# Starting the gathered rows beside the routing, and dealing the rest evenly over the rows of V

## The chip, the cores and the metric

The kernel runs on one core of one Trainium2 chip. Its time is the device time of one execution in microseconds (us); the text before the change has a median of 2013.02 us over three runs (2002.75 to 2023.59). Five engines work side by side, each through its own list of instructions in order: PE (matmul), DVE (elementwise, vector), ACT (activation), POOL (general purpose, also the queue from which indirect gathers are issued) and SP (a queue for plain DMA). An instruction that waits holds up everything behind it on its engine.

## The reference

One layer of a hybrid attention model over 512 latent tokens and 256 context tokens, width 1024, float32. The part that matters here is its last, the PEER expert block. Each token picks, in each of 8 heads, 16 of 16384 experts by product keys, and the block adds up 128 expert outputs for each token:

```python
def block(t):                                   # 128 tokens at a time
    q = (t @ wq).reshape(PEER_BLOCK, PEER_HEADS, 2, PEER_DQ // 2)
    s = jnp.einsum('tpcd,pckd->tpck', q, sub_keys).astype(jnp.float32)
    s1, i1 = lax.top_k(s[:, :, 0], PEER_TOPK)
    s2, i2 = lax.top_k(s[:, :, 1], PEER_TOPK)
    ...                                         # 16 x 16 sums, top 16 of them: idx, top
    g = jax.nn.softmax(top, axis=-1)
    a = jax.nn.gelu(jnp.einsum('tpkd,td->tpk', u[idx], t).astype(jnp.float32), approximate=False)
    return jnp.einsum('tpk,tpkd->td', (g * a).astype(t.dtype), v[idx])
```

`u` and `v` are 16384 x 1024. Ahead of it stand the input projection, neighbourhood attention with a recurrence beside it, and the output projection; behind it a gated residual and an RMSNorm. None of those is touched.

## The kernel before, in words

The first 630 us (projections, mixers, output projection) are left alone by the change. From there on the expert block is one program (`experts`) that treats two groups of tokens in two ways.

- **Tokens 0 to 383, dense.** All 16384 experts are worked through in 128 *rows* of 128 experts. `Activations.step` is one row of U h: the 128x1024 piece of U (`uraw`, fetched two rows at a time) is split into a high and a low part (`uhi` on ACT L66, `ulo` on POOL or DVE L69), PE multiplies both with the tokens in 24 matmuls of 384 columns (`ua`, L396, L397, L399), and ACT applies Gelu (`act`). A row of V is 18 matmuls of 512 columns into `acc` (L555). Its weights are `W` (the softmax weights spread out over experts and tokens) times `act`: POOL multiplies (`w`, L535), ACT and DVE split (`wh`, `wl`), and V itself is split too (`vhi` on ACT, `vlo` on DVE).
- **Tokens 384 to 511, gathered.** For each of 128 slots (8 heads x 16) a 128x1024 tile of rows of U is gathered by index (`rows<-u,gidx`, L417, POOL), DVE takes its dot product with the tokens (L422); after Gelu, the same for rows of V, which DVE adds to `gacc` (L434). These 256 gathers, with `GLAG` = 3 more calls to empty the queue, are 259 *slots* of the generator `gathered`. There are four buffers of `rows`, and a gather is issued three slots ahead of its use. Gathers, dots and sums are kept in program order.

The stages: *retrieval* (`Retrieval.run`: scores and top 16; three steps of U h behind each of the first seven heads), *routing* (`Routing.block`, twelve blocks of 32 tokens, which make `W`: for each of eight groups of four tokens DVE writes one-hot tiles `hot` and `hg` in 16 bit, L348 and L351, PE multiplies them into `wo`, L356, ACT copies them out to `stage`, and SP writes a block's 2 MB to DRAM), then the loop over the *rows of V*, c = 0 to 127. In that loop a row takes a step of U h with it when `up.n < c + 2 * (AHEAD - 1)`, that is while the finished rows of U h are fewer than c + 16; rows with a step are called mixed here, rows without one plain. Rows of U h finished before the loop are spilled to DRAM and fetched back.

What sets the order: a scheduler places each instruction on its engine's list by program order, readiness and its own estimates, and may pull work ahead (steps of the next routing blocks stand before the end of the retrieval on PE). Only what is marked with `keep_in_program_order` keeps the order of the text among itself.

Of the kernel before, what the change touches and what calls it, by code (L numbers as in the profile page):

```python
# [32 lines left out]
P = 128  # L33
# [10 lines left out]
PH, NK, TOPK = 8, 128, 16  # L44
# [114 lines left out]
GRP = 4  # L159
# [250 lines left out]
def gathered(tc, a, pool, gp, idx, weight, h, acc):  # L410

    nc = tc.nc
    dots = pool.tile([P, P], F32, name="dots")

    def rows(src, s):
        t = gp.tile([P, D], F32, name="rows")
        tc.keep_in_program_order(nc.gpsimd.indirect_dma_start(  # L417
            out=t[:], out_offset=None, in_=a[src], in_offset=bass.IndirectOffsetOnAxis(ap=idx[:, s:s + 1], axis=0)))
        return t

    def dot(t, s):
        tc.keep_in_program_order(nc.vector.tensor_tensor_reduce(  # L422
            out=t, in0=t, in1=h, op0=ALU.mult, op1=ALU.add, scale=1.0, scalar=0.0, accum_out=dots[:, s:s + 1]))

    def gelu(sl):
        tc.keep_in_program_order(nc.scalar.activation(out=dots[:, sl], in_=dots[:, sl], func=AF.Gelu))
        nc.vector.tensor_tensor(out=dots[:, sl], in0=dots[:, sl], in1=weight[:, sl], op=ALU.mult)

    def axpy(t, s):
        if s == 0:  # L430
            tc.keep_in_program_order(nc.vector.tensor_scalar(
                out=acc, in0=t, scalar1=dots[:, 0:1], scalar2=None, op0=ALU.mult))
        else:
            tc.keep_in_program_order(nc.vector.scalar_tensor_tensor(  # L434
                out=acc, in0=t, scalar=dots[:, s:s + 1], in1=acc, op0=ALU.mult, op1=ALU.add))

    queue = []
    for n in range(2 * P + GLAG):
        if n in (P // 2 + LATE, P + LATE):
            gelu(slice(n - LATE - P // 2, n - LATE))  # L440
        if len(queue) == GLAG or n >= 2 * P:
            use, t, s = queue.pop(0)
            use(t, s)
        if n < 2 * P:
            s = n % P
            queue.append((dot, rows("u", s), s) if n < P else (axpy, rows("v", s), s))
        yield


GLAG = 3  # L450
# [1 line left out]
LASTV = ((0, 0), (0, 8), (2, 0), (2, 8))  # L452
WQB = 8
AHEAD, UBUFS = 9, 3
RSTEPS, WSTEPS = 3, 2
GRATE = (9, 3)


def experts(tc, ctx, a, dram, ident, modx, h2, hg, xnat):
    nc = tc.nc  # L460
    pool = lambda c, name, bufs, **kw: c.enter_context(tc.tile_pool(name=name, bufs=bufs, reuse_waits="tile", **kw))
    keep = pool(ctx, "pkeep", 1)
    ring = pool(ctx, "ring", AHEAD)
    wctx = ExitStack()
    ups = pool(wctx, "ups", 1, space=PSUM)
    gate_dram = dram.tile([1, D], F32, name="gate_dram")
    nc.sync.dma_start(out=gate_dram.rearrange("o (k p) -> p (o k)", p=P), in_=modx[:, 40:48])
    W = dram.tile([NG, NK, TD // WBLK, GRP * WBLK], F32, name="W")
    idx = keep.tile([P, P], I32, name="gidx")
    weight = keep.tile([P, P], F32, name="gweight")  # L470
    gacc = keep.tile([P, D], F32, name="gacc")
    uctx = ExitStack()
    up = Activations(tc, uctx, a, h2, ring, ups, dram)

    def steps(n):
        for _ in range(n):
            up.step()

    with ExitStack() as c2:
        c2.enter_context(tc.using_default_side("right"))  # L480
        ret = Retrieval(tc, c2, a)
        ret.run(h2, lambda: steps(RSTEPS))
        for g in range(2):
            sl = hg[:, g * 512:(g + 1) * 512]
            t = ups.tile([P, 4, P], F32, name="ut")
            for k in range(4):
                nc.tensor.transpose(out=t[:, k], in_=sl[:, k * P:(k + 1) * P], identity=ident)
            nc.scalar.activation(out=sl, in_=t.rearrange("p k d -> p (k d)"), func=AF.Copy)
        one = pool(c2, "w1", 1)
        eT = one.tile([P, 2, TD], F16, name="eT")  # L490
        gw = one.tile([P, 2, TD], F16, name="gw")
        ps = pool(c2, "wps", 2, space=PSUM)
        rt = Routing(tc, c2, a, ps, eT, gw, W)
        ret.softmax(one)
        for m in range(ND):
            ret.slots(m, one, ps, ident, eT, gw)
        nc.vector.tensor_copy(out=idx, in_=ret.ex[:, ND].rearrange("p h k -> p (h k)"))
        nc.gpsimd.tensor_copy(out=weight, in_=ret.top[:, ND].rearrange("p h k -> p (h k)"))
        for b in range(TD // WBLK):
            steps(WSTEPS)  # L500
            rt.block(b)
        steps(up.n % 2)
    wctx.close()
    up.ps = pool(ctx, "ups", 1, space=PSUM)
    up.ub = 2

    with ExitStack() as c2:
        c2.enter_context(tc.using_default_side("right"))
        vp = pool(c2, "vp", 2)
        gather = gathered(tc, a, keep, pool(c2, "grows", 4), idx, weight, hg, gacc)  # L510

        def more(n):
            for _ in range(n):
                next(gather, None)

        vps = pool(c2, "vps", 1, space=PSUM)
        acc = [vps.tile([P, D], F32, name=f"acc{m}") for m in range(ND)]
        tail = None
        up.lo, up.keep = [nc.vector, nc.gpsimd], NK
        for q in range(AHEAD):  # L520
            up.fetch(q)
        for c in range(NK):
            g, i = divmod(c, GRP)
            if i == 0:
                w = vp.tile([P, TD // WBLK, GRP, WBLK], F32, name="w")
                nc.sync.dma_start(out=w.rearrange("j b i t -> j (b i t)"), in_=W[g].rearrange("j b x -> j (b x)"))
                busy = GRATE[up.n >= c + 2 * (AHEAD - 1)]
            if i % 2 == 0:
                q = c // 2
                up.fetch(q + AHEAD)  # L530
                raw = vp.tile([P, 2, D], F32, name="vraw")
                nc.sync.dma_start(out=raw, in_=a["vP"][q])
                wp = w[:, :, i:i + 2]
                rows = lambda t: t.rearrange("j i (b t) -> j b i t", t=WBLK)
                nc.gpsimd.tensor_tensor(out=wp, in0=wp, op=ALU.mult, in1=rows(up.done[q]))  # L535
                wh = vp.tile([P, 2, TD], F32R, name="wh")
                wl = vp.tile([P, 2, TD], F32R, name="wl")
                split(nc, rows(wh), rows(wl), wp)
                vs = []
            vh = vp.tile([P, D], F32R, name="vhi", bufs=3)  # L540
            vl = vp.tile([P, D], F32R, name="vlo", bufs=3)
            split(nc, vh, vl, raw[:, i % 2])
            vs.append((i % 2, vh, vl))
            more(busy * (i + 1) // GRP - busy * i // GRP)
            if up.n < c + 2 * (AHEAD - 1):
                up.step()
            last = c == NK - 1
            if c == NK - 2:
                continue
            for m in range(ND):  # L550
                sl = slice(m * P, (m + 1) * P)
                for r, vh, vl in vs:
                    for x, y in ((wh, vh), (wh, vl), (wl, vh)):
                        for d in range(2):
                            nc.tensor.matmul(out=acc[m][:, d * 512:(d + 1) * 512], lhsT=x[:, r, sl], rhs=y[:, d * 512:(d + 1) * 512],  # L555
                                             start=(c == 0 and y is vh and x is wh),
                                             stop=(last and r == 1 and x is wl))
            vs = []
            if up.n == NK and tail is None:
                uctx.close()  # L560
                tail = pool(uctx, "tail", 2, side="left")
                ends = final_rows(a, nc, tail, gate_dram)
                xs = [tail.tile([P, D], F32, name=f"tx{m}", bufs=1) for m in range(NT)]
                for m in range(NT):
                    nc.sync.dma_start(out=xs[m], in_=xnat[m * P:(m + 1) * P])
                act_tables(tc, LN_EXP)
        more(2 * P + GLAG)
        for m in (ND, *range(ND)):
            finish(nc, a, tail, ends, xs[m], gacc if m == ND else acc[m], m)
    uctx.close()  # L570


def final_rows(a, nc, pool, gate_dram):

    rows = [pool.tile([P, D], F32, name=n, bufs=1) for n in ("gate", "nf")]
    for t, src in zip(rows, (gate_dram, a["nf"])):
        nc.gpsimd.dma_start(out=t, in_=src.broadcast_to([P, D]))
    return rows
# [650 lines left out]
```

## Time and profile before

| | before |
|---|---|
| median of 3 runs | 2013.02 us (2002.75 to 2023.59) |
| the profiled execution | 2013.56 us, of it a span of 2011.8 us from first to last instruction |
| mean granted PE clock | 0.957 |
| PE busy | 1832.2 us, 91% |
| DVE / POOL / ACT busy | 1443.1 / 954.2 / 760.7 us |
| DMA | 409.11 MB, mean 203 GB/s |

An engine's busy time is a sum over very different stages, so it is to be read stage by stage. The expert block's stages, by the first and last instruction of each on PE: the retrieval ends at 842 us, routing runs from 858.6 to 1042, rows of V from 1065.2 to 1951.6 (plain until 1202.8, mixed until 1867.4, plain again), and after PE has ended the last gathers run until 1991.8 and the residual and norm until 2011.8.

### The profile page before, as it was taken

What the parts mean: (1) busy time and instruction counts of PE and PEld (TensorE: products, weight loads), DVE (VectorE), ACT (ScalarE), POOL (GpSimd) and SP (SyncE); (2) the same over time, 40 slices, a digit from 0 to 9 for tenths busy, and PEclk for the clock granted to TensorE, in tenths of its full rate; (3) what the DMA queues carried; (4) which work ended last, traced back from release to release, by engine and by line L of the source; (5) the groups of instructions that cost most, each with busy time, mean ns of one, the idle gap of its engine ahead of it and who ended that gap; (6) DMA issues with size and microseconds to landing.
All of it is one profiled execution on the core that took longest, in us unless ns stands there. A gap on an engine that the chain in (4) does not pass through costs nothing.

```text
span 2011.8 us, 25393 instructions
## 1 busy us (share of the span) xinstructions
PE 1832.2 (91%) x9501; PEld 1578.0 (78%) x9501; DVE 1443.1 (72%) x2407; ACT 760.7 (38%) x1074; POOL 954.2 (47%) x651
## 2 busy tenths in 40 slices
PE   8999996998899999789988999999999999999870
PEld 4787875776777888688886889999999898888650
DVE  6625385668646799988856677777767777777877
ACT  5322243444435333267653333333333333333311
POOL 2411013333015355622215557767676777677663
PEclk8999997999998999999998999999999999999985
DMA  7317531000134333257778878878787878787885
GB/s 273 100 48 249 190 108 44 9 17 9 48 126 157 109 111 121 86 164 213 225 231 326 335 277 288 304 277 301 269 305 283 299 282 297 279 301 274 333 277 193
DMA packets 140506, 409.11 MB, mean 203 GB/s; under 512 B 11488, under 2 KB 62048, under 8 KB 123488
## 3 DMA queue, kind: packets, MB, share of 16 engines
q1 hardware_dynamic: 93440, 244.20, 34.3%
q0 software_dynamic: 42336, 153.24, 21.9%
q10 hardware_dynamic: 4608, 10.06, 1.3%
q8 instruction: 74, 1.21, 0.2%
q14 instruction: 48, 0.39, 0.1%
HBM read 370.76 MB, written 36.70 MB: 203 GB/s over the span
## 4 chain that ended last, share of the span: by engine, by line
PE 56%; DVE 15%; DMA 14%; issue 9%; POOL 4%; ACT 2%; SPq 0%; POOLq 0%; DVEq 0%; ACTq 0%
PE acc L555 17%; DMA rows<-v,gidx 10%; PE ua L399 6%; PE ua L397 5%; PE ua L396 5%; PE wo L356 3%; PE pj L78 2%; PE pj L77 2%; PE G L817 2%; PE pj L76 2%; DVE gacc L434 2%; POOL rows L417 1%; PE G L881 1%; DVE qk L810 1%; PE qp L78 1%
## 5 line engine op out<-in xcount | busy, mean ns | idle before, releaser
L396 PE MATMUL ua<-h,uhi 128*128 128x384 f32 x1024 | 347.1, 339 | 0.9 <-ACT act L400 0.9
L397 PE MATMUL ua<-h,uhi 128*128 128x384 f32 x1024 | 345.2, 337 | 0.0
L69 POOL TENSOR_TENSOR ulo<-uraw,uhi 128x1024 fp32r<-128x1024 f32 x87 | 213.6, 2458 | 207.4 <-PE ua L399 82.3
L422 DVE CUSTOM_DVE_ANT_0 rows<-rows,hg 128x1024 f32<-128x1024 f32 x128 | 200.0, 1576 | 99.2 <-DMA rows<-u,gidx 99.2
L434 DVE SCALAR_TENSOR_TENSOR gacc<-rows,dots,gacc 128x1024 f32<-128x1024 f32 x127 | 202.4, 1594 | 95.3 <-DMA rows<-v,gidx 93.8
L555 PE MATMUL acc<-vhi,wh 128*128 128x512 f32 x768 | 240.8, 395 | 14.0 <-ACT vhi L66 14.0
L555 PE MATMUL acc<-vlo,wh 128*128 128x512 f32 x768 | 240.5, 394 | 13.7 <-DVE vlo L69 13.7
L66 ACT ACTIVATE uhi<-uraw 128x1024 fp32r<-128x1024 f32 x128 | 135.8, 1062 | 283.4 <-DMA uraw<-uT 168.1
L555 PE MATMUL acc<-vhi,wl 128*128 128x512 f32 x768 | 239.6, 393 | 0.0
L417 POOL DMA_INDIRECT rows<-u,gidx x128 | 200.2, 1564 | 73.2 <-DVE dots L422 51.5
L417 POOL DMA_INDIRECT rows<-v,gidx x128 | 193.7, 1514 | 84.1 <-DVE gacc L434 55.1
L535 POOL TENSOR_TENSOR w<-w,act 128x768 f32<-128x768 f32 x64 | 145.2, 2287 | 144.5 <-DMA w<-W 139.6
L399 PE MATMUL ua<-h,ulo 128*128 128x384 f32 x1024 | 204.7, 338 | 2.8 <-POOL ulo L69 2.8
L396 PEld LDWEIGHTS ua<-h,uhi 128*128 128x128 f32 x1024 | 193.8, 189 | 5.1 <-ACT act L400 1.5
L397 PEld LDWEIGHTS ua<-h,uhi 128*128 128x128 f32 x1024 | 193.5, 189 | 4.2
L66 ACT ACTIVATE vhi<-vraw 128x1024 fp32r<-128x1024 f32 x128 | 134.6, 1054 | 149.8 <-PE acc L555 132.4
L69 DVE TENSOR_TENSOR vlo<-vraw,vhi 128x1024 fp32r<-128x1024 f32 x128 | 170.2, 1332 | 28.6 <-ACT vhi L66 28.6
L555 PEld LDWEIGHTS acc<-vlo,wh 128*128 128x128 f32 x768 | 144.9, 190 | 49.1 <-DVE vlo L69 17.3
L399 PEld LDWEIGHTS ua<-h,ulo 128*128 128x128 f32 x1024 | 179.0, 188 | 5.1 <-POOL ulo L69 5.0
L555 PEld LDWEIGHTS acc<-vhi,wh 128*128 128x128 f32 x768 | 144.4, 189 | 39.4 <-ACT vhi L66 14.3
L555 PEld LDWEIGHTS acc<-vhi,wl 128*128 128x128 f32 x768 | 145.4, 189 | 31.5
L618 DVE TENSOR_TENSOR wlo<-raw,whi 128x1024 fp32r<-128x1024 f32 (+1 forms) x68 | 80.1, 1196 | 93.4 <-ACT whi L615 92.9
(339 smaller groups left out, 3359.1 us busy)
## 6 DMA issues: line engine op xcount, KB each, us to landing
uraw<-uT SPq DMA_DIRECT2D x64, 1024.0 KB
vraw<-vP SPq DMA_DIRECT2D x64, 1024.0 KB
W<-stage SPq DMA_DIRECT2D x12, 2048.0 KB
w<-W SPq DMA_DIRECT2D x32, 768.0 KB
raw<-w_in SPq DMA_DIRECT2D x32, 512.0 KB
sg<-wmB POOLq DMA_DIRECT2D x21, 512.0 KB
raw<-wq SPq DMA_DIRECT2D x32, 256.0 KB
act<-act ACTq DMA_DIRECT2D x16, 384.0 KB
```

Source lines behind the costliest of these rows:

```text
L66: nc.scalar.activation(out=hi, in_=src, func=AF.Copy)
L69: (lo_eng or nc.vector).tensor_tensor(out=lo, in0=src, in1=hi.bitcast(F32), op=ALU.subtract)
L78: nc.tensor.matmul(out=out, lhsT=ll, rhs=rh, start=False, stop=stop and k == n - 1)
L396: nc.tensor.matmul(out=o, lhsT=hi[:, k], rhs=hh[:, k], start=(k == 0), stop=False)
L397: nc.tensor.matmul(out=o, lhsT=hi[:, k], rhs=hl[:, k], start=False, stop=False)
L399: nc.tensor.matmul(out=o, lhsT=lo[:, k], rhs=hh[:, k], start=False, stop=(k == KT - 1))
L417: tc.keep_in_program_order(nc.gpsimd.indirect_dma_start(out=t[:], out_offset=None, in_=a[src], in_offset=bass.IndirectOffsetOnAxis(ap=idx[ ...
L422: tc.keep_in_program_order(nc.vector.tensor_tensor_reduce(out=t, in0=t, in1=h, op0=ALU.mult, op1=ALU.add, scale=1.0, scalar=0.0, accum_out ...
L434: tc.keep_in_program_order(nc.vector.scalar_tensor_tensor(out=acc, in0=t, scalar=dots[:, s:s + 1], in1=acc, op0=ALU.mult, op1=ALU.add))
L535: nc.gpsimd.tensor_tensor(out=wp, in0=wp, op=ALU.mult, in1=rows(up.done[q]))
L555: nc.tensor.matmul(out=acc[m][:, d * 512:(d + 1) * 512], lhsT=x[:, r, sl], rhs=y[:, d * 512:(d + 1) * 512], start=(c == 0 and y is vh and ...
L618: lo_eng.tensor_tensor(out=lo, in0=raw, in1=hi.bitcast(F32), op=ALU.subtract)
```

## The change

1. Five steps of U h are emitted behind the retrieval and four behind the routing (`GAPS`), and a routing block is preceded by three steps instead of two (`WSTEPS`).
2. The generator of gathers is made before the retrieval, with its four buffers on the other side of the memory, and five slots (`WGATHER`) are called behind each routing block: 60 slots before the loop over V begins.
3. In the loop, the fixed numbers of slots for four rows (3 for plain rows, 9 for the others) are replaced by a rate: the remaining 199 slots are dealt so that a mixed row gets four times (`GMIX`) what a plain row gets, and that all are dealt by row 122 (`GEND`). With `up.n` = 66 at that point the rate is 199 / (50 + 4 x 62 + 10) = 0.646 slots for a plain row and 2.58 for a mixed one.

```diff
-RSTEPS, WSTEPS = 3, 2
-GRATE = (9, 3)
+RSTEPS, WSTEPS = 3, 3
+GAPS = (5, 4)
+WGATHER = 5
+GMIX, GEND = 4.0, 122
...
+    grows = pool(ctx, "grows", 4)
...
+    gather = gathered(tc, a, keep, grows, idx, weight, hg, gacc)
+    slots = [0]
+
+    def more(n):
+        for _ in range(n):
+            slots[0] += 1
+            next(gather, None)
...
         ret.run(h2, lambda: steps(RSTEPS))
+        steps(GAPS[0])
...
             steps(WSTEPS)
             rt.block(b)
-        steps(up.n % 2)
+            more(WGATHER)
+        steps(GAPS[1] + up.n % 2)
...
-        gather = gathered(tc, a, keep, pool(c2, "grows", 4), idx, weight, hg, gacc)
...
+        lead = 2 * (AHEAD - 1)
+        plain = max(0, up.n - lead)
+        rate = (2 * P + GLAG - slots[0]) / (plain + GMIX * (NK - lead - plain) + GEND - NK + lead)
+        due = 0.0
...
-                busy = GRATE[up.n >= c + 2 * (AHEAD - 1)]
...
-            more(busy * (i + 1) // GRP - busy * i // GRP)
-            if up.n < c + 2 * (AHEAD - 1):
+            mixed = up.n < min(NK, c + lead)
+            due += rate * (GMIX if mixed else 1)
+            more(int(due))
+            due -= int(due)
+            if mixed:
                 up.step()
```

How the change moves instructions is shown at three places. From line 455 on the changed text's line numbers are higher (L487 is L499, L498 is L510).

First PE at the end of the retrieval: `ua` are matmuls of U h, `ut` transposes of the gathered tokens, `et` the first transposes of the routing's indices, which wait for the retrieval's last results. Before:

```order
L397 MATMUL ua<-h_3985,uhi 128x384
L399 MATMUL ua<-h_3984,ulo 128x384 x8
L396 MATMUL ua<-h_3984,uhi 128x384
L397 MATMUL ua<-h_3985,uhi 128x384
L320 MATMUL et<-ident,rc 128x128
```

and now:

```order
L396 MATMUL ua<-h_3984,uhi 128x384
L499 MATMUL ut<-ident,hg 128x128 x4
L397 MATMUL ua<-h_3985,uhi 128x384
...
L399 MATMUL ua<-h_3984,ulo 128x384 x8
...
L320 MATMUL et<-ident,rc 128x128
```

In both, 27 steps of U h and two matmuls of the 28th stand ahead of the first `et`; only the transposes `ut` moved.

Second POOL through the routing: `ulo` is the low part of a row of U, `rows<-u` a gather, `w` the first multiply of the rows of V. Before:

```order
L498 COPY gweight<-top 128x128
L69 TENSOR_TENSOR ulo<-uraw,uhi 128x1024 x18
L535 TENSOR_TENSOR w<-w,act 128x12x64
L417 DMA rows<-u,gidx 128x1024
L535 TENSOR_TENSOR w<-w,act 128x12x64
```

and now (such clusters of gathers go on until the twelfth block):

```order
L510 COPY gweight<-top 128x128
L69 TENSOR_TENSOR ulo<-uraw,uhi 128x1024
L417 DMA rows<-u,gidx 128x1024 x4
L69 TENSOR_TENSOR ulo<-uraw,uhi 128x1024 x2
L417 DMA rows<-u,gidx 128x1024 x2
L69 TENSOR_TENSOR ulo<-uraw,uhi 128x1024 x4
L417 DMA rows<-u,gidx 128x1024 x5
```

POOL had 18 splits to do in the routing and nothing else; now it has about 36, with clusters of five gathers between them, and two splits and a gather stand close to the first `w`.

Third DVE at the end of a routing block, between the second and the third, with the buffers' numbers. Before, the eight groups of a block and those of the next follow each other:

```order
L351 TENSOR_TENSOR hg_7164<-hot_7162,gw_6764 128x1024
L348 TENSOR_TENSOR hot_7176<-iota16_6776,eT_6763 128x1024
L348 TENSOR_TENSOR hot_7257<-iota16_6776,eT_6763 128x1024
L351 TENSOR_TENSOR hg_7178<-hot_7176,gw_6764 128x1024
L351 TENSOR_TENSOR hg_7259<-hot_7257,gw_6764 128x1024
```

and now:

```order
L348 TENSOR_TENSOR hot_7548<-iota16_6941,eT_6928 128x1024
L351 TENSOR_TENSOR hg_7421<-hot_7419,gw_6929 128x1024
L422 ISA rows_7215,dots_7210<-rows_7215,hg_3986 128x1024
L422 ISA dots_7210 128x1
L422 ISA rows_7218,dots_7210<-rows_7218,hg_3986 128x1024
...
L422 ISA rows_7221,dots_7210<-rows_7221,hg_3986 128x1024
...
L422 ISA rows_7435,dots_7210<-rows_7435,hg_3986 128x1024
...
L351 TENSOR_TENSOR hg_7550<-hot_7548,gw_6929 128x1024
L348 TENSOR_TENSOR hot_7562<-iota16_6941,eT_6928 128x1024
L422 ISA rows_7438,dots_7210<-rows_7438,hg_3986 128x1024
```

Each block now ends on DVE with four dot products, one tile of the next block, and a fifth dot product; each of them waits for its gather, and the next block's tiles stand behind them. In the lists as wholes, 62.8 steps of U h stand ahead of the routing's last `wo` on PE (45.8 before), 67.7 ahead of the first row of V (48.0 before), 52 rows of V ahead of the first mixed one (33 before), 60 mixed rows follow (79 before), and then 16 plain ones, as before. The last gather stands on POOL ahead of the last two multiplies `w`; before, 38 gathers stood behind the last `w`.

## Rows read from the trace of the kernel before

**Rows 1.** View of busy times by stretch; all engines (us, instructions), clock, DMA:
```profile
842.00:858.60 16.60, 0.41 (x2) 0.09 (x1) 16.60 (x20) 2.50 (x4) 10.74 (x7) 0.59 0.24 91
858.60:1042.00 183.40, 176.82 (x1231) 162.52 (x1231) 153.68 (x210) 128.39 (x139) 43.96 (x18) 0.99 0.68 205
1042.00:1065.20 23.20, 8.62 (x49) 8.28 (x48) 6.38 (x5) 5.38 (x8) 8.59 (x5) 0.74 0.91 308
1065.20:1202.80 137.60, 137.55 (x595) 113.05 (x596) 96.69 (x98) 48.81 (x52) 76.58 (x43) 0.98 0.82 308
1202.80:1867.40 664.60, 661.78 (x3343) 599.62 (x3342) 498.76 (x446) 227.55 (x278) 475.93 (x263) 1.00 0.79 289
1867.40:1951.60 84.20, 70.52 (x290) 55.67 (x288) 65.29 (x51) 20.36 (x21) 54.57 (x35) 0.96 0.86 316
1951.60:1991.80 40.20, 0.04 (x1) 0.00 (x0) 27.29 (x22) 0.00 (x0) 21.52 (x18) 0.53 0.76 259
1991.80:2011.80 20.00, 0.00 (x0) 0.00 (x0) 16.02 (x33) 5.93 (x16) 0.00 (x0) 0.50 0.26 105
```

**Rows 2.** The same view, only instructions on `ua` (PE, PEld, ACT), mixed stretch:
```profile
1202.80:1867.40 664.60, 347.75 (x1920) 334.62 (x1919) 38.07 (x79) 1.00 0.79 289
```

**Rows 3.** The same view, only instructions on `acc`, first plain stretch:
```profile
1065.20:1202.80 137.60, 137.55 (x594) 112.82 (x594) 0.00 (x0) 0.98 0.82 308
```

**Rows 4.** Timeline of PE: start, us, instruction, idle before and its releaser:
```profile
828.88 0.33 PE L396 MATMUL ua<-h,uhi 128*128 128x384 f32 x1
833.04 0.33 PE L396 MATMUL ua<-h,uhi 128*128 128x384 f32 x1
...
858.61 0.48 PE L320 MATMUL et<-ident,rc 128*128 128x128 f32 x1 [16.20 <-DVE rc L319]
...
870.11 1.11 PE L356 MATMUL wo<-hg,hot 128*128 128x128 f16 x8 [0.25 <-DVE hg L351]
870.98 0.43 PE L396 MATMUL ua<-h,uhi 128*128 128x384 f32 x1
```

**Rows 5.** Timeline of ACT, the same place in two successive late routing blocks:
```profile
1007.04 1.09 ACT L66 ACTIVATE uhi<-uraw 128x1024 fp32r<-128x1024 f32 x1
...
1023.66 1.10 ACT L66 ACTIVATE uhi<-uraw 128x1024 fp32r<-128x1024 f32 x1
```

**Rows 6.** Timeline of DVE, two groups of a routing block:
```profile
1001.21 1.38 DVE L348 TENSOR_TENSOR hot<-iota,eT 128x1024 f16<-128x1024 f16 x2
1002.50 1.29 DVE L351 TENSOR_TENSOR hg<-hot,gw 128x1024 f16<-128x1024 f16 x2
1003.71 0.68 DVE L348 TENSOR_TENSOR hot<-iota,eT 128x1024 f16<-128x1024 f16 x1
```

**Rows 7.** Timelines of DVE and POOL over the same mixed row of V:
```profile
1257.39 3.58 DVE L422 CUSTOM_DVE_ANT_0 rows<-rows,hg 128x1024 f32<-128x1024 f32 x1 [1.99 <-DMA rows<-u,gidx]
1263.17 1.22 DVE L422 CUSTOM_DVE_ANT_0 rows<-rows,hg 128x1024 f32<-128x1024 f32 x1
1264.31 0.08 DVE L422 DVE_READ_ACCUMULATOR2_ANT dots<- 128x1 f32 x1
...
1257.46 2.42 POOL L69 TENSOR_TENSOR ulo<-uraw,uhi 128x1024 fp32r<-128x1024 f32 x1
1262.10 1.96 POOL L417 DMA_INDIRECT rows<-u,gidx  x1 [0.30 <-issue]
```

**Rows 8.** Busy times by stretch, the last three routing blocks:
```profile
992.00:1042.00 50.00, 49.13 (x338) 45.70 (x336) 37.81 (x46) 34.03 (x37) 12.20 (x5) 1.00 0.72 221
```

**Rows 9.** Groups by line, POOL, 1199 to 1867 us: busy, mean ns, idle before:
```profile
L417 POOL DMA_INDIRECT rows<-u,gidx x104 | 163.8, 1575 | 48.2 <-DVE dots L422 28.8 <-issue 9.5 <-DVE wl L69 3.7
L417 POOL DMA_INDIRECT rows<-v,gidx x80 | 127.5, 1594 | 40.7 <-DVE gacc L434 18.4 <-DVE ulo L69 5.6 <-issue 5.1
L69 POOL TENSOR_TENSOR ulo<-uraw,uhi 128x1024 fp32r<-128x1024 f32 x39 | 94.5, 2422 | 0.7
L535 POOL TENSOR_TENSOR w<-w,act 128x768 f32<-128x768 f32 x40 | 94.4, 2381 | 99.8 <-DMA w<-W 99.8
```

More of the change, by code (lines that the diff above doesn't have):

```diff
@@ L509, in experts @@
         vp = pool(c2, "vp", 2)
-        gather = gathered(tc, a, keep, pool(c2, "grows", 4), idx, weight, hg, gacc)
-        def more(n):
-            for _ in range(n):
-                next(gather, None)
         vps = pool(c2, "vps", 1, space=PSUM)
```

## The prediction

> **What bounds the kernel now.** I read the busy times by stretch first, because the shares of the whole span mix very different stages [rows 1]. From 1065 to 1867 us PE is busy in 799 of 802 us: there only PE's own work counts, and it is the same work before and after. What can be gained lies where PE does not work. There are five such places: 16.6 us between retrieval and routing; 6.6 us inside the routing (183.4 us with 176.8 busy); 23.2 us between routing and rows of V, with 8.6 us busy; 13.7 us in the last plain rows; and the end, 40.2 us of gathers alone and 20.0 us of residual and norm [rows 1]. The end is the plainest: PE has nothing left and POOL issues 18 gathers with their sums behind them. Together that is some 105 us, and the change aims at all five places.
>
> The second thing to read is what one unit costs at full speed. A step of U h starts 4.16 us after the one before it (833.04 - 828.88), and eight `wo` matmuls take 0.87 us, so a block's 64 take 6.96 us [rows 4]. The 594 matmuls of the first plain stretch are 33 rows of V: 137.6 / 33 = 4.17 us for a plain row [rows 3]. The mixed stretch holds 1920 matmuls of U h, that is 80 steps: 664.6 / 80 = 8.31 us for a mixed row [rows 2].
>
> **The change, part by part.** The sum is made against the profiled execution, 2013.56 us, which lies 0.5 us above the median of the three runs; so it stands for the median too.
>
> *Gap before the routing: 0.* The five steps behind the retrieval look as if they filled the 16.2 us in which PE waits for DVE's `rc` [rows 4]. The order says otherwise: the scheduler had already pulled later steps forward, and in both texts 27 steps and two matmuls stand ahead of the first `et`. The same wait ends at the same instruction. I take 0; ends are a gain of 16 if the pull-ahead were enough after all, and a loss of 5 for the one and a third steps that now stand between `et` and the first `wo`.
>
> *Routing: +114.* This is the term that decides. PE must do 62.8 - 27.1 = 35.7 steps there instead of 18.7, three a block: 3 x 4.16 + 6.96 = 19.4 us a block. DVE must do eight groups of `hot` and `hg`, which take 2.50 us for two groups (1003.71 - 1001.21), 10.0 us a block [rows 6], and now five dots of 1.14 us (1264.31 - 1263.17), 5.7 us [rows 7]. And DVE and POOL get in each other's way: a dot that starts together with a split on POOL lasts 3.58 us, the split's 2.42 us plus its own time, 2.36 us more than the dot alone [rows 7]. So the splits count on DVE's side as well: 3 x 2.36 = 7.1 us. That is 22.8 us a block for what cannot run at once on DVE and POOL, above PE's 19.4. In the late blocks before, PE's sum was 2 x 4.16 + 6.96 = 15.3 us and the block took 16.6 us (1023.66 - 1007.04), 9% more than the largest sum, for waits at the seams [rows 5]. The same 9% gives 24.8 us, twelve blocks 298 us, against 183.4: +114. POOL itself has 5 x 1.6 + 3 x 2.4 = 15 us a block, not the bound [rows 9]. The lower end is PE's sum alone, 19.4 us (+50); for the upper one I add the five gathers' POOL time (1.58 us each) to the 22.8, 30.7 us (+185).
>
> Whether a gather belongs into that sum is the open question, and the trace answers it for one case: at 1262.10 a gather is issued on POOL for 1.96 us, and the dot at 1263.17 beside it takes its plain 1.22 us [rows 7]. So I leave it out. The Trainium skill has two sentences on this that pull apart. "SBUF — State Buffer", section "Who interferes with whom", says that a DVE instruction with two inputs in SBUF contends with a POOL instruction that reads SBUF and not with one that only writes it; by that the trace agrees, and the sum stays. Its section "SBUF: two separate sides" warns that POOL cannot write the descriptors of a DMA while DVE runs in a two-port mode; were the 16-bit `hot` and `hg` such a case, the sum would be the upper end, and no run here shows a gather beside them.
>
> *Gap before the rows of V: +1.* Its length is set by the last block's way through memory (W written, read back, multiplied, split), not by PE. The order puts 4.9 steps there, 20.3 us of 23.2, where 2.0 stood. That work is hidden, and is counted below as steps that the mixed rows no longer carry. Two splits and a gather now stand ahead of or beside the first multiply on POOL; at most 5 us, taken as 1, since the multiply waits for DMA meanwhile. PE stays busy, so the clock of 0.74 in this stretch [rows 1] should rise; worth 1 or 2 us, left out.
>
> *Plain rows: +79.* 52 instead of 33: 19 x 4.17. Fewer slots a row than before (0.65 against 0.75), so no new wait.
>
> *Mixed rows: -163.5.* 60.3 steps instead of 80: 19.7 x 8.31. The price of a row is kept although it now carries 2.58 slots instead of 2.25. On POOL a gather cost, with all its waits, (668 - 99.8 - 94.4 - 94.5) / 184 = 2.06 us, and POOL waited 99.8 us for the next `w` [rows 9]. Per row that is 2.58 x 2.06 + 1.18 + 1.18 = 7.7 us, under 8.31. The cover is thin, 0.6 us a row.
>
> *Last plain rows: -17.5.* 16 x 4.17 = 66.7 instead of 84.2: they carried 2.25 gathers each and waited for them; now 0.65, and none after row 122.
>
> *Gathers behind the last matmul: -40.2.* They are dealt out by row 122. Nothing else stands in that stretch [rows 1].
>
> *Residual and norm: -4.0.* One of the four groups of tokens no longer depends on the end: a quarter of DVE's 16.0 us [rows 1].
>
> Sum: 0 + 114 + 1 + 79 - 163.5 - 17.5 - 40.2 - 4.0 = -31. **Forecast: 1982 us.**
>
> **The rivals.**
>
> *Routing at PE's pace.* If the splits fall into DVE's waits (it was idle for 29.7 us of the routing before [rows 1]), the block is 19.4 us plus the same 9%, 21.2 us: 43 us less, 1939 us. For it speaks that the dots stand on DVE where PE runs two steps without a break (8.3 us for 5.7 us of dots). Against it: three splits of 2.4 us have then to fit beside groups that DVE must keep up with.
>
> *Gathers take part in the exclusion (slower).* Place: POOL's clusters of five between the splits, beside `hot` and `hg`. If a gather holds DVE up, or waits for it, the block goes to 30.7 us, +71: 2053 us. The same result comes if dots wait for gathers and gathers for the buffers of dots, one after the other; alone, 18 gathers took 40.2 us, 2.23 us each [rows 1]. It decides from a block of 27.4 us on (24.8 + 31 / 12). Against it speaks the undisturbed dot [rows 7]. [...]
>
> *DMA bounds the routing.* Its share was 0.72 in the late blocks [rows 8], 12.0 us of 16.6. A block now moves 3.34 MB more (five gathers of 0.524, a row of U of 0.524, a spill of 0.197, by their shapes). At the rate of the stretch with the highest share, 308 GB/s at 0.91 [rows 1], that is 9.9 us: 21.9 us in all. At a share of 0.91 that takes 24.1 us, just under 24.8; at the 0.82 of the first plain rows it takes 26.7 us, +23: 2005 us.
>
> *Mixed rows bound by gathers.* If a gather costs 2.45 us instead of 2.06, POOL needs 8.7 us a row, 60 x 0.4 = +23: 2005 us. The alone-price of 2.23 us is still under that (8.1 us).
>
> **How the numbers follow.** Forecast (block of 23 to 26 us) 45%, PE's pace 20%, DMA 13%, mixed rows 10%, gathers in the exclusion 12%. The range leaves out about a tenth at either end: 1938 (PE's pace) to 2022 (between the 2005 of DMA and the 2053 of the slower rival). This kernel's runs tell about 1% from no change: faster means under 1993, slower over 2033. Faster takes most of the forecast, PE's pace and a little of the others, 64%; the same 26%; slower 10%, nearly all of the exclusion.
>
> **What would show it.** The wait before the first `et` still near 16 us; from the first `et` to the last `wo` about 298 us; PE visibly idle inside the routing where it was not before, with DVE near its full share there; 4 or 5 steps in the gap behind it, which stays near 24 us; mixed rows at 8.3 us and the last sixteen at 4.2 us; nothing between the last matmul and the norm but the norm. I am wrong if routing takes under 260 or over 330 us, or if mixed rows cost over 8.6 us.

## The result: slower by 3%

| | median | range of the runs |
|---|---|---|
| before | 2011.66 us | 2002.75 to 2023.59, 4 runs beside the change |
| after | 2074.02 us | 2062.6 to 2085.9, 4 runs |
| ratio | 1.0307 | 95% interval 1.0227 to 1.0387 |

The forecast was 1982 us, in a range of 1938 to 2022. The profiled execution of after took 2085.9 us, 12 us above its median; the terms below are read from it.

First the busy times by stretch of after, cut at the same events as [rows 1]: first `et`, last `wo`, first `acc`, first and last mixed `ua`, last `acc`, end. Columns as there: PE, PEld, DVE, ACT and POOL, each us and (x instructions), then clock, DMA share, GB/s.

```profile
861.66:1210.29 348.63, 261.30 (x1635) 244.49 (x1636) 266.28 (x318) 153.92 (x172) 159.88 (x94) 0.82 0.66 226
1210.29:1240.16 29.87, 21.98 (x119) 21.15 (x117) 9.47 (x9) 9.85 (x14) 16.55 (x10) 0.92 0.93 318
1240.16:1461.60 221.44, 217.41 (x936) 178.20 (x937) 160.19 (x152) 76.48 (x82) 115.89 (x63) 0.98 0.81 305
1461.60:2005.57 543.97, 513.30 (x2530) 461.01 (x2529) 412.98 (x316) 170.26 (x210) 379.37 (x218) 0.98 0.80 285
2005.57:2072.52 66.95, 65.90 (x289) 53.57 (x287) 45.80 (x42) 22.94 (x30) 16.09 (x10) 1.00 0.55 212
2072.52:2084.10 11.58, 0.00 (x0) 0.00 (x0) 7.44 (x18) 2.95 (x8) 0.00 (x0) 0.62 0.34 136
```

| term | forecast | measured against [rows 1] |
|---|---|---|
| up to the first `et` | 0 | +3.1 (861.7 - 858.6) |
| routing | +114 | **+165.2** (348.6 - 183.4) |
| gap before the rows of V | +1 | +6.7 |
| plain rows | +79 | +83.8 |
| mixed rows | -163.5 | **-120.6** (544.0 - 664.6) |
| last plain rows | -17.5 | -17.2 |
| drain, residual and norm | -44.2 | -48.6 (11.6 - 60.2) |
| sum | -31 | +72.4 |

Two terms carry the miss: the routing, 51 us, and the mixed rows, 43. What the change aimed at behind the last matmul came, 4 us better than forecast.

**Where the routing's time goes.** The waits of after, 861.7 to 1210.3 us (engine and line, what it waited for: us in all, times, longest):

```profile
PEld L356 <- DVE hg L351: 93.6, 29, 8.8
PE wo L356 <- DVE hg L351: 85.2, 15, 8.5
...
DVE rows L422 <- DMA rows<-u,gidx: 52.0, 10, 10.2
```

PE stood 85.2 us for `hg` in only 15 waits, so each is long; and DVE, which makes `hg`, itself stood 52 us for gathered rows. At one block's end the chain can be followed, in the timelines of DVE, POOL and PE of after (start, us, instruction, idle before and its releaser):

```profile
1002.89 0.69 DVE L351 TENSOR_TENSOR hg<-hot,gw 128x1024 f16<-128x1024 f16 x1
1005.38 1.23 DVE L422 CUSTOM_DVE_ANT_0 rows<-rows,hg 128x1024 f32<-128x1024 f32 x1 [1.80 <-DMA rows<-u,gidx]
...
1007.74 8.46 DVE L351 TENSOR_TENSOR hg<-hot,gw 128x1024 f16<-128x1024 f16 x2
...
999.81 1.70 POOL L417 DMA_INDIRECT rows<-u,gidx  x1 [10.43 <-DVE dots L422]
...
1006.89 1.15 POOL L417 DMA_INDIRECT rows<-u,gidx  x1 [0.61 <-DVE dots L422]
1008.06 6.98 POOL L69 TENSOR_TENSOR ulo<-uraw,uhi 128x1024 fp32r<-128x1024 f32 x3
...
1015.65 1.11 PE L356 MATMUL wo<-hg,hot 128*128 128x128 f16 x8 [5.67 <-DVE hg L351]
```

Read it from the top. The block's five gathers stand together on POOL, and the first waits 10.43 us for a dot that frees a buffer. The dot at 1005.38 waits 1.80 us for the row asked for at 999.81; with DVE in order, the next block's `hot` and `hg` stand behind it. The fifth gather waits for that dot too, and the block's three splits stand behind it on POOL. So the splits run together at 1008.06, 6.98 us, exactly when DVE makes the next block's first `hg`: a pair that takes 1.29 us alone [rows 6] takes 8.46. PE, without `hg`, stands for 5.67 us.

Here the row was late only because it was asked for late: it came 5.6 us after its gather was issued (999.81 to 1005.38), while the DMA engines were half busy. In the block before it was worse. Timelines of DVE, POOL and SP of after, 960 to 986 us:

```profile
982.06 1.23 DVE L422 CUSTOM_DVE_ANT_0 rows<-rows,hg 128x1024 f32<-128x1024 f32 x1 [8.06 <-DMA rows<-u,gidx]
...
971.84 1.78 POOL L417 DMA_INDIRECT rows<-u,gidx  x1
...
969.19 0.38 SPq L359 DMA_DIRECT2D W<-stage  x1
971.72 3.24 SPq L388 DMA_DIRECT2D uraw<-uT  x1
```

There the block's `W` store and a load of U are issued just ahead of the gather, its row comes after 10.2 us (971.84 to 982.06), and PE stands 6.3 us and then 4.5 for `hg`. U is fetched two rows at a time and a block takes three, so the two patterns take turns: of the 52.0 us that DVE stood for rows, five waits of 8 to 10 us make 42.8 and five of 1.8 to 1.9 us the rest. The DMA in stretches of after around these two blocks' ends (columns as above):

```profile
971.84:982.06 10.22, 5.79 (x36) 5.33 (x35) 2.16 (x5) 3.49 (x5) 4.60 (x4) 0.88 1.02 316
999.81:1005.38 5.57, 5.57 (x35) 5.57 (x34) 3.78 (x7) 3.25 (x5) 4.65 (x4) 1.00 0.54 146
1003.00:1021.00 18.00, 12.33 (x74) 11.55 (x73) 14.49 (x12) 5.83 (x7) 10.80 (x7) 0.81 1.02 359
1021.00:1030.00 9.00, 8.91 (x63) 8.40 (x62) 8.06 (x14) 7.03 (x8) 1.71 (x1) 1.00 0.01 3
1012.00:1015.00 3.00, 0.00 (x0) 0.00 (x0) 3.00 (x1) 0.00 (x0) 3.00 (x2) 0.78 1.02 367
1015.00:1018.00 3.00, 2.35 (x13) 2.35 (x14) 3.00 (x5) 1.09 (x1) 0.04 (x1) 0.50 1.11 363
```

The DMA engines are full from 1003 to 1021, when the block's `W` store, the next rows of U and the gathers all run, and idle (0.01) for the nine microseconds behind. The mean share of 0.66 says nothing of that. The clock column shows a second cost: 0.50, that is 1.2 GHz, right after PE's stand.

**Where the mixed rows' time goes.** Groups by line of after, 1490 to 2000 us (busy us, mean ns, idle before):

```profile
L399 PE MATMUL ua<-h,ulo 128*128 128x384 f32 x448 | 93.4, 352 | 30.1 <-POOL ulo L69 30.1
...
L399 PEld LDWEIGHTS ua<-h,ulo 128*128 128x128 f32 x448 | 81.2, 196 | 35.5 <-POOL ulo L69 35.5
```

PE waited 30 us for POOL's `ulo`. Per row (24 matmuls of `ua` each) the price rose with the gathers dealt to it: 8.31 us at 2.25 gathers before, 9.02 at 2.58 now (543.97 us for 60.3 rows).

### The profile page after: what moved, and what is told of

Same layout as the page of the kernel before. It is cut to its first block, busy times and chain, and to the rows that moved or that the text cites. A ratio compares the mean times of both kernels' runs of the same rounds, so it can differ in the third digit from the quotient of the medians.

```text
span 2084.1 us, 25358 instructions
## 1 busy us (share of the span) xinstructions
PE 1857.2 (89%) x9501; PEld 1597.0 (77%) x9501; DVE 1479.9 (71%) x2397; ACT 760.9 (37%) x1074; POOL 961.7 (46%) x661
## 3 DMA queue, kind: packets, MB, share of 16 engines
q8 instruction: 74, 1.21, 0.2%
## 4 chain that ended last, share of the span: by engine, by line
PE 41%; issue 16%; DMA 15%; DVE 15%; POOL 9%; ACT 3%; SPq 0%; POOLq 0%; DVEq 0%; ACTq 0%
PE acc L568 11%; DMA rows<-v,gidx 6%; POOL rows L417 4%; POOL ulo L69 3%; DMA rows<-u,gidx 3%; PE ua L399 3%; PE ua L396 3%; PE ua L397 3%; PE wo L356 2%; DVE hg L351 2%; DMA w<-W 2%; PE G L830 2%; PE pj L78 1%; PE pj L77 1%; PE G L894 1%
## 5 line engine op out<-in xcount | busy, mean ns | idle before, releaser
L396 PE MATMUL ua<-h,uhi 128*128 128x384 f32 x1024 | 357.6, 349 | 3.0 <-ACT act L400 3.0
L397 PE MATMUL ua<-h,uhi 128*128 128x384 f32 x1024 | 353.7, 345 | 0.0
L69 POOL TENSOR_TENSOR ulo<-uraw,uhi 128x1024 fp32r<-128x1024 f32 x97 | 241.9, 2506 | 128.3 <-PE ua L399 89.1
L434 DVE SCALAR_TENSOR_TENSOR gacc<-rows,dots,gacc 128x1024 f32<-128x1024 f32 x127 | 209.9, 1652 | 96.3 <-DMA rows<-v,gidx 95.3
L417 POOL DMA_INDIRECT rows<-u,gidx x128 | 175.2, 1369 | 189.5 <-DVE dots L422 157.4
L422 DVE CUSTOM_DVE_ANT_0 rows<-rows,hg 128x1024 f32<-128x1024 f32 x128 | 194.5, 1546 | 88.4 <-DMA rows<-u,gidx 88.4
L568 PE MATMUL acc<-vhi,wh 128*128 128x512 f32 x768 | 242.2, 397 | 8.4 <-ACT vhi L66 8.4
L568 PE MATMUL acc<-vlo,wh 128*128 128x512 f32 x768 | 240.2, 394 | 1.6 <-DVE vlo L69 1.4
L568 PE MATMUL acc<-vhi,wl 128*128 128x512 f32 x768 | 239.7, 394 | 0.0
L399 PE MATMUL ua<-h,ulo 128*128 128x384 f32 x1024 | 209.6, 345 | 30.7 <-POOL ulo L69 30.1
L399 PEld LDWEIGHTS ua<-h,ulo 128*128 128x128 f32 x1024 | 183.4, 193 | 36.6 <-POOL ulo L69 35.5
L545 POOL TENSOR_TENSOR w<-w,act 128x768 f32<-128x768 f32 x64 | 144.2, 2270 | 137.1 <-DMA w<-W 88.7
L396 PEld LDWEIGHTS ua<-h,uhi 128*128 128x128 f32 x1024 | 200.5, 196 | 6.1 <-ACT act L400 3.4
L397 PEld LDWEIGHTS ua<-h,uhi 128*128 128x128 f32 x1024 | 199.9, 195 | 3.2
L356 PE MATMUL wo<-hg,hot 128*128 128x128 f16 x768 | 102.9, 297 | 85.8 <-DVE hg L351 85.2
L568 PEld LDWEIGHTS acc<-vhi,wh 128*128 128x128 f32 x768 | 146.4, 192 | 36.0 <-ACT vhi L66 9.7
L568 PEld LDWEIGHTS acc<-vlo,wh 128*128 128x128 f32 x768 | 145.9, 190 | 35.5 <-DVE vlo L69 3.6
L568 PEld LDWEIGHTS acc<-vhi,wl 128*128 128x128 f32 x768 | 145.6, 190 | 31.3
```

What stands on the lines that cost most here:

```text
L69: (lo_eng or nc.vector).tensor_tensor(out=lo, in0=src, in1=hi.bitcast(F32), op=ALU.subtract)
L356: nc.tensor.matmul(out=o[:, t], lhsT=hot[:, 1, :, t], rhs=hg[:, i, :, t], start=(i == 0), stop=(i == 1))
L396: nc.tensor.matmul(out=o, lhsT=hi[:, k], rhs=hh[:, k], start=(k == 0), stop=False)
L397: nc.tensor.matmul(out=o, lhsT=hi[:, k], rhs=hl[:, k], start=False, stop=False)
L399: nc.tensor.matmul(out=o, lhsT=lo[:, k], rhs=hh[:, k], start=False, stop=(k == KT - 1))
L417: tc.keep_in_program_order(nc.gpsimd.indirect_dma_start(out=t[:], out_offset=None, in_=a[src], in_offset=bass.IndirectOffsetOnAxis(ap=idx[ ...
```

## The experiments

Each was timed in three rounds beside the kernel before. "Routing" is from the first `et` to the last `wo` in the profile. In the changed text `acc` is L568 and the multiply `w` L545; in e10, e13, e14 and e15 the numbers behind the new line in `block` are one higher (L422 is L423).

| run | median us | ratio to before, 95% | routing us | mixed row us |
|---|---|---|---|---|
| after | 2074.0 | 1.0307 (1.0227 to 1.0387) | 348.6 | 9.02 |
| e1 no gathers in routing | 2040.5 | 1.0130 (1.0072 to 1.0188) | 251.6 | 9.78 |
| e2 two rows a block | 2057.5 | 1.0204 (1.0129 to 1.0279) | 307.8 | 8.47 |
| e4 DVE splits in routing | 2050.5 | 1.0185 (1.0101 to 1.0269) | 330.8 | 8.8 |
| e11 copies | 2049.3 | 1.0166 (1.0127 to 1.0205) | 253.8 | 10.0 |
| e12 dots | 2080.3 | 1.0328 (1.0289 to 1.0368) | 287.5 | 9.9 |
| e10 spread | 1997.9 | 0.9927 (0.9883 to 0.9971) | 279.7 | 8.8 |
| e13 cluster mid-block | 2034.2 | 1.0122 (1.0074 to 1.0171) | 317.5 | 8.8 |
| e5 DVE splits in mixed rows | 2031.7 | 1.0084 (1.0051 to 1.0116) | 347.5 | 8.28 |
| e6 step before gathers | 2097.8 | 1.0415 (1.0364 to 1.0466) | 345.9 | 9.2 |
| e8 e1 and e5 | 2020.0 | 1.0022 (0.9984 to 1.0061) | 251.7 | 9.3 |
| **e14 e10 and e5** | **1960.4** | **0.9745 (0.9708 to 0.9783)** | 281.1 | 8.23 |
| e15 e14 and e4 | 1957.8 | 0.9737 (0.9699 to 0.9775) | 277.0 | 8.23 |

### The gathers or the third row

e1 edits after:

```diff
-WGATHER = 5
+WGATHER = 0
```

> Leaves the three steps of U h a block, the steps in the gaps and the new dealing as they are, but no gather stands in the routing; its 60 go into the rows of V (0.86 a plain row and 3.43 a mixed row instead of 0.66 and 2.64). Theory A (clusters of gathers on POOL hold the splits up, which then run back to back beside DVE's hg): without them a block is near PE's 19.4 us and a ninth part for seams, routing 255 to 275 us instead of 349. The mixed rows then carry more gathers ahead of POOL's splits and lose 36 to 84 us: 2030 to 2080 us in all. Theory B (three splits a block are too many beside hot and hg, with or without gathers): routing stays at 320 to 350 us, 2110 us or more.

e2:

```diff
-RSTEPS, WSTEPS = 3, 3
+RSTEPS, WSTEPS = 3, 2
```

> Two steps of U h a routing block instead of three; the five gathers a block stay. Theory A (the gathers): PE still stands behind late splits, routing 265 to 295 us; some 12 steps more in the mixed rows at 9.1 - 4.2 = 4.9 us each, 2055 to 2075 us in all. Theory B (the third step): routing back at 195 to 215 us, about -140 + 59, 1990 us.

Busy times by stretch, the routing of e1:

```profile
858.25:1109.87 251.62, 247.84 (x1635) 234.19 (x1636) 166.23 (x209) 154.31 (x172) 87.94 (x37) 0.99 0.63 196
```

PE is busy in 247.8 of 251.6 us, 21.0 us a block. Against [rows 1] it does 404 matmuls more (1635 - 1231), 16.8 steps of 4.16 us [rows 4]: 70 us, and the stretch is 68 longer. The added rows cost their own matmuls and nothing else, and Theory B falls; Theory A's range began 3 us higher. (The shares in the expectation, 3.43 gathers a mixed row and 2.64 in after, are slightly high: the code deals 259 / 308 x 4 = 3.36, and 2.58 in after.) The 60 gathers cost 97 us with three rows a block (348.6 - 251.6). With two they cost about 84: e2's routing holds 1462 matmuls, 9.6 steps or 40 us more than before, and is 124 us longer; that is 13 us beyond Theory A's 295, and the total, 2057.5, lies in its range all the same, because a mixed row cost 8.47 us and not 9.1. The same 1635 matmuls kept PE busy for 261.3 us in after: 13 of the 97 us are its lower clock.

### Whose splits, whose bytes, whose dots

e4 puts `up.lo = [nc.vector]` ahead of the loop over blocks.

> All splits of U in the routing are made by VectorE; gathers, steps and dealing stay. Theory A (a split late on POOL and DVE's hg shut each other out): POOL carries gathers alone; DVE has 10.0 + 5.7 + 3 x 1.2 = 19.3 us a block, PE 19.4: routing 255 to 280 us, 1980 to 2010 us in all. Theory C (dots wait for late gathers and gathers for the four buffers; POOL's splits only fill that time): DVE still stands for the rows, routing 320 us or more, 2045 us or more.

Its waits in the routing, 855.8 to 1186.6 us:

```profile
ACT uhi L66 <- DMA uraw<-uT: 67.1, 10, 9.4
...
PE ua L396 <- ACT uhi L66: 51.6, 8, 9.2
...
PE wo L356 <- DVE hg L351: 5.5, 6, 3.1
```

A miss for Theory A in the size: without a split on POOL the wait for `hg` is nearly gone, 5.5 us, and the routing still takes 330.8. Theory C has the time, but not its sign: DVE stood only 12.3 us for gathered rows. PE stands 51.6 us for `uhi` instead, and ACT, which makes it, for U's rows from memory. Their loads stood on SP for DVE, 93 us in eight waits between 900 and 1100 us: DVE, with its splits behind its dots, frees their two buffers late, and they then load while the DMA is busy with the `W` store and the gathers. One such load in e4's timelines of SP and ACT:

```profile
1012.73 3.08 SPq L388 DMA_DIRECT2D uraw<-uT  x1
...
1026.24 2.00 ACT L66 ACTIVATE uhi<-uraw 128x1024 fp32r<-128x1024 f32 x2 [6.42 <-DMA uraw<-uT]
```

So the shut-out was one form that the delay took; with it gone, 79 of the 97 us stay in another (330.8 - 251.6).

Next, two halves of a gather, each alone, both on e1. e11 moves the bytes, which nobody waits for; e12 does the dots on a buffer that is always there. The copies and the fixed dots are additions to the program; their results are used nowhere.

```diff
+            for j in range(COPIES):                     # e11, 5 a block
+                r = b * COPIES + j
+                tc.keep_in_program_order(nc.gpsimd.dma_start(out=pad[r], in_=a["vP"][r][:, 0]))
```

> The kernel without gathers in the routing, with five copies of 0.5 MB a block from memory to memory on POOL's queue in their place, which nobody waits for: the bytes of the gathers without dots, buffers or waits. Theory D (bytes at the block's end): PE comes to wait for rows of U, routing 285 to 330 us. Theory A (DVE's dots and the splits): 250 to 265 us.

```diff
+            for j in range(DOTS):                       # e12, 5 a block
+                tc.keep_in_program_order(nc.vector.tensor_tensor_reduce(
+                    out=junk, in0=fill, in1=hg, op0=ALU.mult, op1=ALU.add, scale=1.0, scalar=0.0, accum_out=jd[:, j:j + 1]))
```

> The kernel without gathers in the routing, with five dots a block on a fixed buffer: DVE's work of the gathers without their bytes. Theory A, as forecast (10.0 + 5.7 + 3 x 2.36 = 22.8 us a block that DVE and POOL cannot do at once, and 9%): 285 to 300 us of routing. Theory D: 252 to 268 us.

The routing's stretch of e11, then of e12:

```profile
859.52:1113.35 253.83, 248.67 (x1635) 235.13 (x1636) 164.16 (x209) 154.28 (x172) 116.12 (x94) 0.99 0.96 315
```

```profile
861.11:1148.65 287.54, 259.48 (x1635) 244.04 (x1636) 265.62 (x324) 153.39 (x172) 95.47 (x37) 0.89 0.55 171
```

The bytes alone cost 2 us, at a DMA share of 0.96: the rival that bandwidth binds the routing falls, and Theory D in the form written there (PE waiting for U) with it. The dots alone cost 36 us, 24.0 us a block, where the forecast's sum had 24.8. So of the 97 us some 38 are the two halves, and about 59 appear only when the two are joined: when a dot has to wait for its row and a gather for a dot to free its buffer. That is a difference of runs, which takes the halves to add up.

### Where the gathers stand

e10 hands `more` to `block` and calls it behind each group:

```diff
+            more(g % 8 in (2, 3, 4, 5, 6))
...
-            more(WGATHER)
```

> The five gathers of a block stand one behind each of its groups 2 to 6 instead of together behind the last. Theory D (a block's W store, rows of U and gathers all start at its end, fill the DMA engines for 18 to 20 us, and then leave them idle for 10; what lands last holds DVE or PE up): the gathers fall into the idle part, routing 265 to 300 us. Theory A (a sum on DVE and POOL, 22.8 us and its seams): 298 us or more, and nothing changes by the place, near 349 us.

e13 has `more(5 * (g == 3))` in that place.

> The five gathers of a block stay together but stand behind its group 3, half a block away from the W store and the next block's first hg. If what costs is the place (five rows asked for when the W store fills the DMA engines, their dots ahead of the next block's hg): routing 280 to 300 us, near the 279.7 of the spread ones. If it is the cluster (four buffers, three rows ahead: five in a row cannot all be under way, wherever they stand): 325 to 350 us.

The routing's stretch of e10, and DVE's wait for rows in that of e13; in e10's answer on waits there is no such row.

```profile
867.59:1147.30 279.71, 257.09 (x1661) 238.66 (x1662) 257.54 (x323) 159.75 (x174) 165.73 (x98) 0.97 0.88 291
```

```profile
DVE rows L423 <- DMA rows<-u,gidx: 26.8, 11, 3.2
```

Spread, the same 60 gathers cost 28 us instead of 97 (279.7 - 251.6; 4.5 of the 28 are 26 matmuls more that the order puts into this stretch), and DMA's share rises from 0.66 to 0.88. e13's 317.5 us lies between its two cases, so both causes that it should part are real: the cluster moved half a block off gains 31 us, spreading it 38 more. DVE's wait for rows orders all three: 52.0, 26.8 and none, for 348.6, 317.5 and 279.7 us. By itself it doesn't measure the loss, as e4's 12.3 us with 330.8 show. More than four buffers of rows were not tried.

### The mixed rows

e5 has all splits of the rows of V on DVE:

```diff
-        up.lo, up.keep = [nc.vector, nc.gpsimd], NK
+        up.lo, up.keep = [nc.vector], NK
```

> All splits of U in the rows of V are made by VectorE instead of every second one by POOL; the routing stays. Theory A2 (a mixed row costs 9.1 us because POOL's split stands behind five or six gathers whose issue waits for dots and sums): mixed rows 8.3 to 8.5 us, 35 to 48 us less, 2025 to 2040 us. Theory B2 (DVE is what the gathers fill up; 28 splits more on it make it worse): mixed rows 9.1 us or more, 2070 to 2100 us.

e6 keeps POOL's share and writes the step ahead of the row's gathers:

```diff
+            if mixed:
+                up.step()
             more(int(due))
             due -= int(due)
-            if mixed:
-                up.step()
```

> In the mixed rows of V the step of U h is written ahead of the row's gathers; every second split stays on POOL, and the routing stays. If a mixed row costs 9.1 us because POOL's split stands behind gathers: 8.4 to 8.7 us, 2035 to 2055 us in all. If it is the split on POOL as such, or the number of gathers: 9.0 us or more, 2070 us or more.

e5 comes out as Theory A2 had it, 42 us under after; from 1236 to 1950 us PE is busy in 711 of 714. The stretch:

```profile
1236.23:1950.47 714.24, 711.43 (x3460) 628.40 (x3459) 559.80 (x494) 253.18 (x290) 419.17 (x252) 1.00 0.84 314
```

e6 is a plain miss. First one group of after, 1600 to 1800 us, then two of e6 in the same window:

```profile
L399 PE MATMUL ua<-h,ulo 128*128 128x384 f32 x175 | 36.4, 350 | 12.9 <-POOL ulo L69 12.9
```

```profile
L568 PE MATMUL acc<-vlo,wh 128*128 128x512 f32 x129 | 41.5, 403 | 13.1 <-DVE vlo L69 13.1
...
L399 PE MATMUL ua<-h,ulo 128*128 128x384 f32 x176 | 34.5, 337 | 2.3 <-POOL ulo L69 2.3
```

And a moment in e6's timelines of DVE and POOL:

```profile
1654.94 3.37 DVE L69 TENSOR_TENSOR vlo<-vraw,vhi 128x1024 fp32r<-128x1024 f32 x1
...
1659.09 1.21 DVE L69 TENSOR_TENSOR vlo<-vraw,vhi 128x1024 fp32r<-128x1024 f32 x1
...
1654.50 2.72 POOL L69 TENSOR_TENSOR ulo<-uraw,uhi 128x1024 fp32r<-128x1024 f32 x1
```

The wait for `ulo` is nearly gone, and one for `vlo` has come: POOL's split now runs beside the split of V, which takes 3.37 us instead of 1.21. So the place on POOL's list explains the wait of after, but a better place is no cure; taking the split off POOL is.

### The repairs together

> No gather in the routing, and all splits of U in the rows of V on VectorE. If the two losses are separate (gathers in the routing, 97 us between 348.6 and 251.6; POOL's split behind gathers in the mixed rows), both go: routing 250 to 255 us, rows of V with PE full, some 785 us: 1925 to 1955 us in all, faster than both kernels. If the 60 gathers more in the rows of V bind them (POOL 256 x 2.06 + 64 x 2.4 = 681 us of 785, so with little to spare), they take 820 us or more: 1970 us or more.

e8 (e1's and e5's edits) came out as its second case: its 2020.0 us lie 65 above the first one's range, and the rows of V took 864 us. At 3.36 gathers a mixed row they lose even with POOL free of splits (9.3 us a row; POOL waited 99 us for dots and 79 for sums between 1140 and 1950 us). The prices of a mixed row with POOL's splits, 8.31 us at 2.25 gathers, 8.47 at 2.31 (e2), 8.8 to 9.0 at 2.58, 9.78 at 3.36 (e1), show how soon it begins. So part of the gathers has to begin in the routing, and e14 keeps that: e10's and e5's edits.

> The two repairs together: the routing's gathers spread through the block, and U's splits in the rows of V on VectorE. Routing 280 us, gap 25, rows of V 782 us with PE full, end 12 us: 1945 to 1970 us, faster than both kernels. If the repairs share a cause, or the rows of V lose again: 1985 us or more.

Its routing and its mixed rows, by stretch:

```profile
859.54:1140.65 281.11, 259.43 (x1661) 241.12 (x1662) 259.01 (x323) 159.81 (x174) 166.81 (x98) 0.96 0.87 289
...
1387.99:1882.02 494.03, 494.03 (x2504) 449.46 (x2503) 399.04 (x344) 175.13 (x207) 298.46 (x188) 1.00 0.85 318
```

1960.4 us, 2.5% under before: all parts of the change are kept, only the gathers' places and the splits' engine differ, and PE is busy without a gap through the mixed rows. e15 adds e4's edit.

> As the run with both repairs, with the routing's splits on VectorE too. If what is left of the routing's loss (279.7 against 251.6 us) is POOL's splits shutting DVE out (3 x 2.36 us of the 22.8): DVE 10.0 + 5.7 + 3 x 1.2 = 19.3 us, routing 252 to 265 us, 1925 to 1950 us. If rows of U come late because VectorE frees their buffers late (67 us of waits for them in the run with clusters and VectorE's splits): routing 290 us or more, 1970 us or more.

It came between its two cases, 277.0 us of routing, and its time is that of e14 within the intervals. The shut-out is gone (`hot` and `hg` take 689 and 687 ns on the mean, in e14 1204 and 818), and 16.8 us of PE's waits for `uhi` have taken the place of 18.5 for `hg`.

## Why the prediction was wrong

**The routing (+114, came +165).** The failed step is "So I leave it out", which took the gather out of the sum and left 9% "for waits at the seams" to stand for all waiting. The sum of work itself was sound: e12, which has just that work, took 287.5 us where it said 298. But a dot was priced as 1.14 us of work, not as a wait for a row that POOL may ask for only when an earlier dot has freed a buffer. Five slots in a row with four buffers, in every second block behind a `W` store and a load of U that fill the DMA, close a ring through POOL, DMA and DVE, and the next block's `hot`, `hg` and splits stand in the same lists. The waits were 27% on top of the sum (29.1 us a block against 22.8), not 9%.

The slower rival had this in its second sentence ("dots wait for gathers and gathers for the buffers of dots, one after the other"), at 30.7 us a block; after has 29.1. That the two are close is luck: the 30.7 adds up POOL's time for five gathers and prices no wait. I gave it 12% because of the undisturbed dot of [rows 7], which speaks only against its first half, that a gather shuts DVE out. That half is indeed false, as e15's timelines of DVE and POOL show, with a gather beside `hg` and a dot:

```profile
1005.79 0.69 DVE L351 TENSOR_TENSOR hg<-hot,gw 128x1024 f16<-128x1024 f16 x1
1006.39 1.22 DVE L423 CUSTOM_DVE_ANT_0 rows<-rows,hg 128x1024 f32<-128x1024 f32 x1
...
1006.14 1.14 POOL L418 DMA_INDIRECT rows<-u,gidx  x1 [1.81 <-DVE dots L423]
```

All take their plain time, and over e15's whole routing `hg` keeps its 0.69 us (687 ns on the mean). The Trainium skill's warning in "SBUF — State Buffer", "SBUF: two separate sides", on descriptors that POOL cannot write, is for a DVE in a two-port mode; no run here shows the 16-bit `hot` and `hg` to be such a case.

**The mixed rows (-163.5, came -120.6).** The failed step is "Per row that is ... 7.7 us, under 8.31". It compared POOL's work with the row's length. PE does not wait for POOL's work of a row, but for one split in every second row, and that stood behind five or six gathers. With a list in order, the place counts. Of the 43 us, 30 are PE's waits for `ulo`; the rest is PE's own longer time (busy for 513.3 us over 60.3 rows, against 661.8 over 80 [rows 1]: 8.51 and 8.27 us a row) at a granted clock of 0.98 instead of 1.00.

Both conditions named for being wrong were met: a routing over 330 us and mixed rows over 8.6.

**The small terms.** The gap before the routing kept its end (3.1 us later, for the same `rc`), but not by the sign named: the wait ahead of `et` was 7.28 us instead of near 16, because PE had by then already stood 5.17 us ahead of the transposes `ut`. The plain rows, the last sixteen and the drain came as forecast. The norm gained 8.4 us (20.0 - 11.6), twice the quarter that was counted. The gap before the rows of V lost 6.7 us, more than the 5 given as its bound: from the last `W` store to its reading back SP's list shows 15.3 us instead of 10.4 (issued at 1211.55 and 1226.87, before at 1042.30 and 1052.74). Without gathers in the routing (e1) the gap was 25.5 us instead of 29.9. The five places add up to 111.7 us, not "some 105"; nothing in the forecast used that sum. PE's pace, the first rival, is what three rows a block cost without gathers: 251.6 us for its 12 x 21.2 = 254.

## What to carry to other kernels

When work with a latency (a gather and its use) is moved into a stage, follow one of its items through every in-order list it enters, and ask what stands behind it there; a sum of busy times per engine is only the lower end. Hand such work out one piece at a time, and ask at what point of the period the transfers start: a mean DMA share of 0.66 in after was 1.0 for about two thirds of a block and near 0 for most of the rest. And before work is put on an engine because it has time left, look which wait on another engine would end there.

## What the runs showed of the hardware

- Splits back to back on POOL kept a two-input DVE instruction out until the last had ended: in after two `hg` took 8.46 us beside three splits of 6.98. The record of `hg` even begins 0.3 us ahead of POOL's first split (1007.74 and 1008.06). The Trainium skill, "SBUF — State Buffer", "SBUF: two separate sides", says that whichever of the two starts first gets the shared ports for the whole instruction; by these records the one that began first came last.
- With copies beside the routing the DMA engines moved 315 GB/s at a share of 0.96, and the stage took 2 us longer (e11): nearly full DMA engines did little harm to a stage that waits for none of the added bytes.
- A gathered row of 0.5 MB came 5.6 us after its issue with the DMA at a share of 0.54, and after 10.2 us at 1.02 (after, 999.81 and 971.84).
- A PE stand of 5.67 us was followed by a granted clock of 0.50 (1.2 GHz) in the next three microseconds. Over the routing of after the lower clock made the same matmuls 13 us longer.
